# First head's rotation of two of three groups on VectorE, the high/low split of later heads asked for later, queries and keys low part first

## The chip, the cores and the metric

The kernel runs on one core of one Trainium2 chip. The metric is the time of one execution on the device in microseconds (us); of several runs the median counts. A core has five engines that run side by side, each with its own queue, which it works off in order: TensorE (PE; its weight loads PEld) multiplies matrices into PSUM, VectorE (DVE) and ScalarE (ACT) do elementwise work, GpSimd (POOL) too, but from SBUF alone here, and SyncE (SP) issues the transfers from HBM.

## What is computed

A decoder trunk of two layers over 256 tokens of width 1024. Layer 0 mixes tokens by a short gated convolution, layer 1 by dilated window attention; each is followed by a squared-ReLU MLP (1024 to 4096 and back) and a gated per-layer embedding. The change is in layer 1's attention, cut here to what matters:

```python
def dilated_attention_mixer(h, positions, w_qkv, w_o):       # 3 groups x 8 heads of 128
    qkv = (h @ w_qkv).reshape(b_, s_, 3, g_ * hh, dh)
    q = partial_rotary(qkv[:, :, 0], positions).reshape(b_, s_, g_, hh, dh)
    k = partial_rotary(qkv[:, :, 1], positions).reshape(b_, s_, g_, hh, dh)
    v = qkv[:, :, 2].reshape(b_, s_, g_, hh, dh)
    for g, (window, dilation) in enumerate(((128, 1), (512, 4), (2048, 16))):
        o_g, lse_g = dilated_window_attention(q[:, :, g], k[:, :, g], v[:, :, g], window, dilation)
    ...
    weights = jax.nn.softmax(jnp.stack(lses, axis=0), axis=0)
    o = jnp.sum(weights[..., None] * jnp.stack(outs, axis=0), axis=0)
    return o.reshape(b_, s_, hh * dh) @ w_o

def partial_rotary(x, positions):                            # the first 32 of a head's 128
    return concatenate([x1 * cos - x2 * sin, x2 * cos + x1 * sin, xf[..., ROPE_DIM:]])
```

## The kernel before

**Arithmetic.** Activations lie with channels on the partitions and tokens along the free dimension (`[128, 2, 256]` for two blocks of 128 channels). To keep float32 accuracy every operand of a large product is split into a high part, rounded to float32r, and a low part, the rest: ScalarE copies the high part (`whi` of weights, L332; activations in `split_into`, L405), VectorE subtracts (`wlo`, L281). A product is low weight times high activation plus high weight times both. In `block` (L343), for kind "w", that is two matmuls: `wlo` with 256 columns, and `whi` with 512 (high and low activation side by side), into one PSUM bank; `sums` (L381) adds the bank's halves at the end, ScalarE copying one half (L385), VectorE adding the other (L386). For the half `i` = 0 (queries) `wlo` comes first, for `i` = 1 (keys) `whi` (L358).

**Weights** come from HBM in slabs of 1024 columns (`raw`), five ahead; slab `si` + 5 is split when slab `si` is first used (`LOOK`). A head's queries and keys are two slabs per group, six in all, then four slabs of 768 columns for its values.

**The plan.** `make_plan` (L134) writes the order of all work as one list: matmul blocks, and steps (`("do", name, ...)`) between them. Instructions are recorded in this order, a scheduler puts them on each engine's queue by it, and waits are set where data is passed on. For the attention the plan goes head by head (L185 to L191): queries and keys of group 0, 1, 2 (`qk`; a group is 32 matmuls), each followed by `add_up` (out of PSUM) and `qk_out`; then values (`v`, 48 matmuls). The scores, the transposes (`turn`) and the product with the values (`values`) of head h - 1 stand between the blocks of head h. Head 0 is apart (L173 to L180): its three groups are accumulated side by side in three banks while the last gate is still being finished, then `add_up` of all three, the first two value blocks, `spread(3)` (which multiplies the norm's reciprocal into the tables `cosr` and `sinr`, L494 and L495), `qk_out` of the three groups, and the rest of the values. Head 1 is `late`: `scores(0)` stands after its third group, `turn(0)` after six of eight value steps, so 36 matmuls behind the scores.

**Rotation.** `qk_out(head, g)` (L607) is four GpSimd operations over query and key of a group, `t` of `[128, 512]`: times `cosr` (L609), two multiplies of 16 rows by `sinr` into the scratch tile `rot[g % 2]` (L612), and an addition of 48 rows (L618). For g = 0 it then asks for the split of `t` (`split_into`, L621), since group 0's scores are computed from high and low parts (L641); groups 1 and 2 go into the scores as they are (L644).

**Softmax of a head's scores** (`scores`, L635): VectorE adds the mask and takes the maximum (L647), negates it, ScalarE takes the exponential (L651; its table is loaded once before), VectorE the reciprocal, ScalarE scales (L653). `turn` (L656) transposes the result on TensorE (`tp`, L662).

Of the kernel before, what the change touches and what calls it, by code (L numbers as in the profile page):

```python
# [9 lines left out]
F32 = mybir.dt.float32  # L10
# [3 lines left out]
ALU = mybir.AluOpType  # L14
# [4 lines left out]
NK = D // P  # L19
# [3 lines left out]
GROUPS = 3  # L23
# [110 lines left out]
def make_plan():  # L134
    plan = [("do", "begin")]
    plan += proj_plan()
    for c in range(NP):
        for s, what in ((1, "C"), (2, "X"), (0, "B")):
            for k in range(NK):
                for i in (0, 1):  # L140
                    kind = "w" if what == "X" else "n"
                    plan.append((kind, "sc_in", k, s * NK + 2 * c + i, (what, c), i, "x0"))
                if c == 0 and (what, k) in ((("C", 3), ("C", 7), ("X", 1), ("X", 3))):
                    plan.append(("do", "squares", 0, (3, 7, 1, 3).index(k) if what == "C" else 2 + (k == 3)))
                if (c, what, k) == (0, "B", 2):
                    plan.append(("do", "stat", 0))
                if (c, what, k) == (1, "C", 4):
                    plan += [("do", "spread", 0), ("do", "conv", 0)]
            if what == "X":
                plan.append(("do", "add_up", (what, c)))  # L150
        if c:
            plan.append(("do", "conv", c))

    def mix(key, j, ks):
        return [("n", key, k, 2 * j + i, ("o", j), i, "y") for k in ks for i in (0, 1)]

    for k in range(6):
        plan += mix("sc_out", 0, (k,)) + mix("sc_out", 1, (k,))
    for j in range(NP):
        plan += mix("sc_out", j, range(6 if j < 2 else 0, NK)) + [("do", "mix_out", 0, j)]  # L160
    plan += mlp_plan(0) + gate_plan()

    plan.append(("do", "masks"))

    def qk(h, g, ks):
        return [
            ("w" if h else "n", "qkv", k, (i, g, h), ("qk", h, g), i, "x3") for k in ks for i in (0, 1)
        ]

    def v(h, ks):  # L170
        return [("t", "v", k, h, ("v", b, h), b, "x3") for k in ks for b in (0, 1)]

    for kp in range(NP):  # L173
        if kp == NP - 1:
            plan.append(("do", "stat", 3))
        for g in range(GROUPS):
            plan += qk(0, g, (2 * kp, 2 * kp + 1))
    plan += [("do", "add_up", ("qk", 0, g)) for g in range(GROUPS)]
    plan += v(0, (0, 1)) + [("do", "spread", 3)]
    plan += [("do", "qk_out", 0, g) for g in range(GROUPS)] + v(0, range(2, NK)) + [("do", "v_out", 0)]  # L180

    def sums(h, g):
        return [("do", "add_up", ("qk", h, g)), ("do", "qk_out", h, g)]

    for h in range(1, HEADS):  # L185

        late, steps = h == 1, [[("do", what, h - 1)] for what in ("scores", "turn", "values")]
        plan += qk(h, 0, range(NK)) + ([("do", "values", 0)] if h == 2 else []) + sums(h, 0)
        plan += [] if late else steps[0]
        plan += qk(h, 1, range(NK)) + sums(h, 1) + qk(h, 2, range(NK)) + steps[late ^ 1] + sums(h, 2)  # L190
        plan += v(h, range(6)) + steps[2 - late] + v(h, range(6, NK)) + [("do", "v_out", h)]  # L191

    last = HEADS - 1
    plan += [x for k in (0, 1, 2) for j in range(NP) for x in mix("w_o", j, (k,))]
    plan.append(("do", "scores", last))
    plan += [x for k in (3, 4) for j in range(NP) for x in mix("w_o", j, (k,))]
    plan.append(("do", "turn", last))
    plan += [x for k in (5, 6) for j in range(NP) for x in mix("w_o", j, (k,))]
    plan.append(("do", "values", last))
    for j in range(NP):  # L200
        plan += mix("w_o", j, (7,)) + [("do", "mix_out", 1, j)]
    plan += mlp_plan(1) + [("do", "last_load")] + last_plan()
    return plan
# [36 lines left out]
def tile_trunk(ctx: ExitStack, tc: tile.TileContext, plan, slabs, ap, out):  # L240
    nc = tc.nc
# [7 lines left out]
    def const(shape, name, dtype=F32):  # L249
        return cpool.tile(shape, dtype, tag=name, name=name)  # L250
# [4 lines left out]
    def held(tag, name, bufs=1, dtype=F32):  # L255
        return cpool.tile([P, 2, S], dtype, tag=tag, bufs=bufs, name=name)

    def pair(name, tag="pair", dtype=F32R):

        if tag == "pair":  # L260
            t = apool.tile([P, 2, 2, S], dtype, tag=tag, bufs=PAIR_BUFS, name=name)
        else:
            t = cpool.tile([P, 2, 2, S], dtype, tag=tag, bufs=1, name=name)
        return t[:, :, 0, :], t[:, :, 1, :], t
# [4 lines left out]
    def both(t):  # L269
        return t.unsqueeze(1).to_broadcast([P, 2, S])  # L270
# [17 lines left out]
    cosr = const([P, S], "cosr")  # L288
    sinr = const([P, S], "sinr")
    rot = [const([P, 2, S], f"rot{n}") for n in range(2)]  # L290
    pos = const([P, S], "pos", I32)
    h = [held("h", f"h{j}", NP + 1) for j in range(NP)]
    state = {k: {} for k in ("u", "y", "p0", "p1", "qk", "pT", *(f"x{n}" for n in range(6)))}
    acc, left, opened = {}, {}, set()
    for op in plan:
        if op[0] != "do":
            key = ((*op[4], op[5]), 0) if op[0] == "w" else (op[4], op[5] if op[0] == "n" else 0)
            left[key] = left.get(key, 0) + 1
    rstd, diags, rows, cur, mask, by_token = {}, {}, {}, {}, {}, {}
# [43 lines left out]
    def block(kind, key, k, col, name, half, operand, m=0, cuts=1):  # L343
        name = (*name, half) if kind == "w" else name
        if name not in opened:
            acc[name] = bank("acc_" + "_".join(map(str, name)))
        left[name, half if kind == "n" else 0] -= 1
        whi, wlo = weights((key, k, col))
        x = state[operand][k // 2]
        if kind == "n":  # L350
            dst = acc[name][:, half, :]
            products = ((dst, wlo, x[0][:, k % 2, :]), (dst, whi, x[1][:, k % 2, :]), (dst, whi, x[0][:, k % 2, :]))
        elif kind == "w":

            dst = acc[name]
            products = ((dst[:, 0, :], wlo, x[0][:, k % 2, :]), (flat(dst), whi, flat(x[2][:, k % 2, :, :])))

            products = products[::-1] if half else products  # L358
        else:
            n = width(key) * P // cuts  # L360
            whi, wlo = (t[:, m * n : (m + 1) * n] for t in (whi, wlo))
            dst = flat(acc[name])[:, :n]
            xhi, xlo = (t[:, k % 2, half * P : (half + 1) * P] for t in x[:2])
            products = ((dst, xhi, whi), (dst, xhi, wlo), (dst, xlo, whi))
        for n, (to, a, b) in enumerate(products):
            nc.tensor.matmul(  # L366
                to,
                a,
                b,
                start=n == 0 and name not in opened,  # L370
                stop=n == len(products) - 1 and left[name, half if kind == "n" else 0] == 0,
                skip_group_check=True,
            )
            opened.add(name)

    def close(name):
        opened.discard(name)

        return acc.pop(name)
# [21 lines left out]
    def split_into(kind, j, src, cuts=1):  # L401
        hi, lo, t = pair(f"{kind}{j}", "pp" if kind in ("p0", "p1") else "pair")
        for n in range(cuts):
            i = slice(2 * n // cuts, 2 * (n + 1) // cuts)
            nc.scalar.activation(hi[:, i, :], src[:, i, :], AF.Copy)  # L405
            sub(lo[:, i, :], src[:, i, :], hi[:, i, :])
        state[kind][j] = (hi, lo, t)
# [197 lines left out]
        h_ready(3, j)  # L605

    def qk_out(head, g):  # L607
        p, t = cur["qk", head, g]
        nc.gpsimd.tensor_tensor(t, p, both(cosr), ALU.mult)  # L609
        r = rot[g % 2]  # L610
        for src, dst in ((32, 0), (0, 32)):
            nc.gpsimd.tensor_tensor(  # L612
                r[dst : dst + 16],
                p[src : src + 16],
                sinr[src : src + 16].unsqueeze(1).to_broadcast([16, 2, S]),
                ALU.mult,
            )
        nc.gpsimd.tensor_tensor(t[:48], t[:48], r[:48], ALU.add)  # L618
        cur["qk", head, g] = t
        if g == 0:  # L620
            split_into("qk", head, t)  # L621

    def v_out(head):

# [130 lines left out]
    def last_scale(b, c):  # L755
# [6 lines left out]

    steps = dict(
        begin=begin, add_up=add_up, squares=squares, proj_out=proj_out, stat=stat, stat_rows=stat_rows, conv=conv, mix_out=mix_out, up_out=up_out,
        down_out=down_out, gate_out=gate_out, rope=rope, masks=masks_load, qk_out=qk_out, v_out=v_out,
        scores=scores, turn=turn, spread=spread, values=values,
        last_load=last_load, turn_h=turn_h, last_gate=last_gate, last_out=last_out, last_rms=last_rms, last_scale=last_scale,
    )
# [95 lines left out]
```

## Time and profile before

| | us |
|---|---|
| runs, median of 3 | 795.62 (795.31 to 795.94) |
| the profiled execution | 797.34 |
| its span, first to last instruction | 795.5 |
| TensorE busy in it | 776.2 (98%) |
| VectorE / ScalarE / GpSimd busy | 582.1 / 436.6 / 177.2 |
| head 1, up to head 2's first matmul (336.7 to 373.8 us) | 37.1 |
| each later head | 29.2 |

The profile is one execution. Its page sums the busy time of each engine; the views of the trace list instructions in order of time with the idle time before each and what ended it (`<-`), the waits of one engine on another, and the busy time and granted clock of a stretch. Times are from the start of the span. Layer 0 lasts to about 323 us, head 0's products overlap its end, heads 1 to 7 run to 550 us, and the second MLP, gate and last norm to the end.

### The profile page before, as it was taken

To read this page: it belongs to the slowest core of one execution; us is meant where nothing else is said; L and a number is where in the kernel's file an instruction comes from. 1 tells how busy PE (TensorE), PEld (TensorE's weight loads), DVE (VectorE), ACT (ScalarE), POOL (GpSimd) and SP (SyncE) were. 2 spreads that over 40 slices of the span, in tenths; PEclk is the share of its full clock that TensorE was granted. 3 is DMA by queue.
4 is the path that set the end of the run, shared out by engine and by line. 5 is a ranking of instruction groups with operands and counts; after the bars stand their busy time and mean duration, and the time that the engine had idled before them with its cause. 6 is when DMAs were issued, how large, how long until landed. Compare 5 with 4: busy or idle time off the path is not lost.

```text
span 795.5 us, 12797 instructions
## 1 busy us (share of the span) xinstructions
PE 776.2 (98%) x4986; PEld 711.6 (89%) x4986; DVE 582.1 (73%) x818; ACT 436.6 (55%) x672; POOL 177.2 (22%) x117
## 2 busy tenths in 40 slices
PE   8999999999999999996999999999999999999996
PEld 7999998888888999986999999999988888888985
DVE  6987789898556669747678679679598887555555
ACT  7654565565444447527647546646475555444453
POOL 0000000000000000298587677678000000000001
PEclk9999999999999999998999999999999999999999
DMA  8866555656556555643464455456556655555521
GB/s 277 287 211 193 183 187 181 198 187 196 185 186 188 185 163 168 203 128 115 150 186 144 154 180 159 159 159 200 174 159 189 198 188 191 185 185 189 184 78 54
DMA packets 41676, 140.98 MB, mean 177 GB/s; under 512 B 4752, under 2 KB 5136, under 8 KB 41616
## 3 DMA queue, kind: packets, MB, share of 16 engines
q1 hardware_dynamic: 41616, 140.17, 55.7%
q8 instruction: 39, 0.64, 0.3%
q14 instruction: 21, 0.17, 0.1%
HBM read 139.10 MB, written 1.05 MB: 176 GB/s over the span
## 4 chain that ended last, share of the span: by engine, by line
PE 87%; DVE 5%; POOL 3%; ACT 2%; issue 2%; DMA 1%; SPq 0%; POOLq 0%; DVEq 0%; ACTq 0%
PE acc_d L366 23%; PE acc_u L366 22%; PE acc_qk L366 13%; PE acc_v L366 7%; PE acc_o L366 6%; PE acc_g L366 5%; PE acc_B L366 2%; PE acc_X L366 2%; DVE wlo L281 2%; PE acc_C L366 2%; POOL rot L612 2%; PE tp L662 1%; PE o L683 1%; PE sc L644 1%; ACT whi L332 1%
## 5 line engine op out<-in xcount | busy, mean ns | idle before, releaser
L281 DVE TENSOR_TENSOR wlo<-raw,whi 128x1024 fp32r<-128x1024 f32 (+3 forms) x273 | 364.5, 1343 | 130.0 <-ACT whi L332 127.9
L332 ACT ACTIVATE whi<-raw 128x1024 fp32r<-128x1024 f32 (+3 forms) x273 | 276.3, 1018 | 201.4 <-PE acc_d L366 82.0
L366 PE MATMUL acc_d<-u,whi 128*128 128x512 f32 (+1 forms) x640 | 166.8, 351 | 0.0
L366 PE MATMUL acc_u<-x,whi 128*128 128x512 f32 x512 | 161.0, 396 | 0.0
L366 PE MATMUL acc_qk<-x,whi 128*128 128x512 f32 (+1 forms) x432 | 122.9, 371 | 0.0
L438 POOL TENSOR_TENSOR n<-v,power 128x4 f32<-128x4 f32 (+1 forms) x6 | 6.5, 1085 | 512.2 <-DVE v L458 509.4
L366 PEld LDWEIGHTS acc_u<-x,wlo 128*128 128x128 f32 x512 | 96.4, 188 | 22.4
L366 PEld LDWEIGHTS acc_d<-u,wlo 128*128 128x128 f32 x512 | 96.9, 189 | 17.0
L366 PE MATMUL acc_d<-u,wlo 128*128 128x256 f32 x512 | 111.8, 279 | 0.0
L366 PE MATMUL acc_u<-x,wlo 128*128 128x256 f32 x512 | 101.3, 278 | 0.0
L366 PEld LDWEIGHTS acc_d<-u,whi 128*128 128x128 f32 x640 | 98.5, 190 | 0.0
L612 POOL TENSOR_TENSOR rot<-qk,sinr 16x512 f32<-16x512 f32 x48 | 87.0, 1813 | 3.3
L366 PEld LDWEIGHTS acc_qk<-x,wlo 128*128 128x128 f32 x384 | 72.4, 188 | 14.2
L366 PE MATMUL acc_qk<-x,wlo 128*128 128x256 f32 x384 | 82.5, 281 | 0.0
L366 PEld LDWEIGHTS acc_u<-x,whi 128*128 128x128 f32 x512 | 78.0, 189 | 0.1
L366 PE MATMUL acc_v<-whi,x 128*128 128x384 f32 x256 | 69.8, 343 | 0.0
L366 PEld LDWEIGHTS acc_qk<-x,whi 128*128 128x128 f32 x432 | 66.1, 189 | 0.0
L609 POOL TENSOR_TENSOR qk<-qk,cosr 128x512 f32<-128x512 f32 x24 | 37.9, 1578 | 57.9 <-DVE qk L386 44.6
L366 PEld LDWEIGHTS acc_v<-whi,x 128*128 128x128 f32 x256 | 47.4, 191 | 0.0
L366 PE MATMUL acc_o<-y,whi 128*128 128x256 f32 x256 | 46.0, 284 | 0.0
L366 PE MATMUL acc_v<-wlo,x 128*128 128x384 f32 x128 | 43.3, 339 | 0.0
L618 POOL TENSOR_TENSOR qk<-qk,rot 48x512 f32<-48x512 f32 x24 | 42.8, 1784 | 1.7
(164 smaller groups left out, 1029.6 us busy)
## 6 DMA issues: line engine op xcount, KB each, us to landing
raw<-in_w SPq DMA_DIRECT2D x232, 512.0 KB, 3.7
raw<-in_w SPq DMA_DIRECT2D x32, 384.0 KB, 3.1
raw<-in_w SPq DMA_DIRECT2D x7, 256.0 KB, 5.7
h<-in_xT SPq DMA_DIRECT2D x4, 256.0 KB, 6.0
out<-ht SPq DMA_DIRECT2D x4, 256.0 KB, 2.0
pt<-in_pT SPq DMA_DIRECT2D x2, 256.0 KB, 4.6
mask<-in_mask SPq DMA_DIRECT2D x2, 256.0 KB, 4.3
gain<-in_gain SPq DMA_DIRECT2D x2, 256.0 KB, 4.2
```

What stands on the lines that cost most here:

```text
L281: nc.vector.tensor_tensor(out, a, f32(b), ALU.subtract)
L332: nc.scalar.activation(hi[:, :width], t[:, :width], AF.Copy)
L366: nc.tensor.matmul(to, a, b, start=n == 0 and name not in opened, stop=n == len(products) - 1 and left[name, half if kind == "n" else 0] == 0,
L438: nc.gpsimd.tensor_tensor(y, v, power[:, : v.shape[1]], ALU.pow)
L609: nc.gpsimd.tensor_tensor(t, p, both(cosr), ALU.mult)
L612: nc.gpsimd.tensor_tensor(r[dst : dst + 16], p[src : src + 16], sinr[src : src + 16].unsqueeze(1).to_broadcast([16, 2, S]), ALU.mult,)
L618: nc.gpsimd.tensor_tensor(t[:48], t[:48], r[:48], ALU.add)
L644: nc.tensor.matmul(ps[:, (g + 1) * P : (g + 2) * P], t[:, 0, own], t[:, 1, own], start=True, stop=True)
L662: nc.tensor.transpose(ps[n // 2][:, n % 2, b * P : (b + 1) * P], sm[:, n * P : (n + 1) * P], ident)
L683: nc.tensor.matmul(ps[:, 0, b * P : (b + 1) * P], v12[:, b, g * P : (g + 1) * P], t[:, g, b * P : (b + 1) * P], start=False, stop=g == 1, ...
```

## The change

Four edits, all in the attention. The first head's groups 0 and 1 are no longer copied out of PSUM by ScalarE; `qk_out` finds their bank still open and does the same four operations on VectorE, reading PSUM (`engine`). Group 2 is copied and rotated on GpSimd as before, first of the three in the plan. The scratch tile is `rot[0]` for groups 0 and 1 and `rot[1]` for group 2. The split of group 0 is a step of its own, `qk_split`: for head 0 it stands after the first sums of head 1, for head h from 1 on after three of eight value steps instead of right after `qk_out(h, 0)`. And `block` no longer turns the order round for the keys.

```diff
-    plan += [("do", "add_up", ("qk", 0, g)) for g in range(GROUPS)]
+    plan.append(("do", "add_up", ("qk", 0, 2)))
     plan += v(0, (0, 1)) + [("do", "spread", 3)]
-    plan += [("do", "qk_out", 0, g) for g in range(GROUPS)] + v(0, range(2, NK)) + [("do", "v_out", 0)]
+    plan += [("do", "qk_out", 0, g) for g in (2, 0, 1)] + v(0, range(2, NK)) + [("do", "v_out", 0)]
...
-        plan += [] if late else steps[0]
+        plan += [("do", "qk_split", 0)] if late else steps[0]
         plan += qk(h, 1, range(NK)) + sums(h, 1) + qk(h, 2, range(NK)) + steps[late ^ 1] + sums(h, 2)
-        plan += v(h, range(6)) + steps[2 - late] + v(h, range(6, NK)) + [("do", "v_out", h)]
+        plan += v(h, range(3)) + [("do", "qk_split", h)] + v(h, range(3, 6)) + steps[2 - late]
+        plan += v(h, range(6, NK)) + [("do", "v_out", h)]
...
-            products = products[::-1] if half else products
+            products = products[::-1] if half and key != "qkv" else products
...
     def qk_out(head, g):
-        p, t = cur["qk", head, g]
-        nc.gpsimd.tensor_tensor(t, p, both(cosr), ALU.mult)
-        r = rot[g % 2]
+        if ("qk", head, g) in acc:
+            engine, p, t = nc.vector, close(("qk", head, g)), pair(f"qk_{head}_{g}", dtype=F32)[1]
+        else:
+            engine, (p, t) = nc.gpsimd, cur["qk", head, g]
+        engine.tensor_tensor(t, p, both(cosr), ALU.mult)
+        r = rot[g // 2]
         for src, dst in ((32, 0), (0, 32)):
-            nc.gpsimd.tensor_tensor(
+            engine.tensor_tensor(
...
-        nc.gpsimd.tensor_tensor(t[:48], t[:48], r[:48], ALU.add)
+        engine.tensor_tensor(t[:48], t[:48], r[:48], ALU.add)
         cur["qk", head, g] = t
-        if g == 0:
-            split_into("qk", head, t)
+
+    def qk_split(head):
+        split_into("qk", head, cur.pop(("qk", head, 0)))
```

What this does to VectorE's queue behind `cosr` and `sinr` is seen first of before, then of the change. In the names `qk_0_1` is head 0, group 1, `acc_...` its PSUM bank, `qk0` and `qk1` the split of a head's group 0; the last number is the tile's own.

```order
L494 TENSOR_TENSOR cosr_78<-cosr_78,row_3_3694 128x256
L495 TENSOR_TENSOR sinr_79<-sinr_79,row_3_3694 128x256
L281 TENSOR_TENSOR wlo124_3734<-raw124_3588,whi124_3733 128x1024
L281 TENSOR_TENSOR wlo125_3752<-raw125_3635,whi125_3751 128x1024
L281 TENSOR_TENSOR qk0_3702<-qk_0_0_3665,qk0_3702 128x2x256
L630 SCALAR_TENSOR_TENSOR v0_0_3767<-acc_v_0_0_3671,n2_3_3613,v0_0_3767 128x128
L630 SCALAR_TENSOR_TENSOR v0_0_3767<-acc_v_1_0_3681,n2_3_3613,v0_0_3767 128x128
```

```order
L495 TENSOR_TENSOR cosr_78<-cosr_78,row_3_3690 128x256
L496 TENSOR_TENSOR sinr_79<-sinr_79,row_3_3690 128x256
L613 TENSOR_TENSOR qk_0_0_3698<-acc_qk_0_0_3465,cosr_78 128x2x256
L616 TENSOR_TENSOR rot0_80<-acc_qk_0_0_3465,sinr_79 16x512 x2
L613 TENSOR_TENSOR qk_0_1_3703<-acc_qk_0_1_3484,cosr_78 128x2x256
L622 TENSOR_TENSOR qk_0_0_3698<-qk_0_0_3698,rot0_80 48x2x256
L282 TENSOR_TENSOR wlo124_3729<-raw124_3588,whi124_3728 128x1024
L616 TENSOR_TENSOR rot0_80<-acc_qk_0_1_3484,sinr_79 16x512 x2
L282 TENSOR_TENSOR wlo125_3747<-raw125_3635,whi125_3746 128x1024
```

Eight operations of the rotation come in ahead of and between the two weight splits, and head 0's split leaves this place.

On ScalarE, from a weight copy of the second head to the table load of the first exponential, of before and then of the change:

```order
L332 ACTIVATE whi129_3859<-raw129_3749 128x768
L405 ACTIVATE qk1_3830<-qk_1_0_3821 128x2x256
L385 ACTIVATE qk_1_1_3879<-acc_qk_1_1_0_3833 128x256
L332 ACTIVATE whi130_3891<-raw130_3776 128x768
L385 ACTIVATE qk_1_1_3879<-acc_qk_1_1_1_3842 128x256
L332 ACTIVATE whi131_3914<-raw131_3799 128x1024
L385 ACTIVATE qk_1_2_3964<-acc_qk_1_2_0_3888 128x256
L332 ACTIVATE whi132_3976<-raw132_3834 128x1024
L385 ACTIVATE qk_1_2_3964<-acc_qk_1_2_1_3897 128x256
L651 ACT_TABLE_LOAD
```

```order
L333 ACTIVATE whi129_3854<-raw129_3744 128x768
L386 ACTIVATE qk_1_1_3874<-acc_qk_1_1_0_3828 128x256
L386 ACTIVATE qk_1_1_3874<-acc_qk_1_1_1_3837 128x256
L333 ACTIVATE whi130_3886<-raw130_3771 128x768
L333 ACTIVATE whi131_3909<-raw131_3794 128x1024
L386 ACTIVATE qk_1_2_3959<-acc_qk_1_2_0_3883 128x256
L406 ACTIVATE qk1_4000<-qk_1_0_3816 128x2x256
L386 ACTIVATE qk_1_2_3959<-acc_qk_1_2_1_3892 128x256
L333 ACTIVATE whi132_3971<-raw132_3829 128x1024
L656 ACT_TABLE_LOAD
```

The split of head 1 (`qk1`) moves from ahead of the sums of groups 1 and 2 to between the two sums of group 2, still ahead of the table load.

## Rows read from the trace of the kernel before

**Rows 1.** The page, busy us, share of the span and instructions of TensorE

```profile
PE 776.2 (98%) x4986; PEld 711.6 (89%) x4986; DVE 582.1 (73%) x818; ACT 436.6 (55%) x672; POOL 177.2 (22%) x117
```

**Rows 2.** TensorE's waits in the whole program: us in total, times, longest

```profile
PE tp L662 <- ACT sm L653: 7.0, 1, 7.0
```

**Rows 3.** TensorE in order of time, second head: start us, us, engine, line, operation

```profile
353.43 0.51 PE L641 MATMUL sc<-qk 128*128 128x256 f32 x3
...
355.35 0.42 PE L366 MATMUL acc_v<-whi,x 128*128 128x384 f32 x1
...
368.81 1.97 PE L662 MATMUL tp<-ident,sm 128*128 128x128 f32 x8 [6.97 <-ACT sm L653]
370.43 0.67 PE L366 MATMUL acc_v<-whi,x 128*128 128x384 f32 x1
...
373.78 0.28 PE L366 MATMUL acc_qk<-x,wlo 128*128 128x256 f32 x1
```

**Rows 4.** The same view, a later head: scores and transposes

```profile
410.10 0.51 PE L641 MATMUL sc<-qk 128*128 128x256 f32 x3
...
411.62 0.36 PE L366 MATMUL acc_qk<-x,wlo 128*128 128x256 f32 x1
...
422.87 1.04 PE L662 MATMUL tp<-ident,sm 128*128 128x128 f32 x8
423.66 0.42 PE L366 MATMUL acc_v<-whi,x 128*128 128x384 f32 x1
```

**Rows 5.** The chain that ended last, in order of time: start us, us, what

```profile
382.71 11.16 PE acc_qk L366 x64
...
423.91 6.24 PE acc_v L366 x36
...
431.75 2.08 PE acc_v L366 x12
...
439.76 0.45 PE sc L644 x4
```

**Rows 6.** Stretch: us, busy PE, PEld, DVE, ACT, POOL, then granted clock, DMA

```profile
370.40:372.90 2.50, 2.50 (x10) 2.50 (x9) 2.50 (x2) 2.50 (x4) 2.42 (x2) 0.50 0.00 0
```

**Rows 7.** GpSimd, ScalarE, VectorE in order of time, heads 0 and 1

```profile
333.28 1.34 POOL L609 TENSOR_TENSOR qk<-qk,cosr 128x512 f32<-128x512 f32 x1 [7.95 <-DVE cosr L494]
...
334.69 4.38 POOL L612 TENSOR_TENSOR rot<-qk,sinr 16x512 f32<-16x512 f32 x2
...
358.26 1.27 POOL L618 TENSOR_TENSOR qk<-qk,rot 48x512 f32<-48x512 f32 x1
359.56 0.63 ACT L405 ACTIVATE qk<-qk 128x512 fp32r<-128x512 f32 x1 [12.07 <-POOL qk L618]
...
360.23 0.69 DVE L281 TENSOR_TENSOR qk<-qk,qk 128x512 fp32r<-128x512 f32 x1 [8.47 <-ACT qk L405]
```

**Rows 8.** ScalarE in order of time, ahead of head 0's exponentials

```profile
362.57 1.06 ACT L332 ACTIVATE whi<-raw 128x1024 fp32r<-128x1024 f32 x1
...
363.93 1.28 ACT L651 ACT_TABLE_LOAD   x1
365.22 0.72 ACT L651 ACTIVATE sm<-sm,st 128x512 f32<-128x512 f32 x1
```

**Rows 9.** VectorE's groups by form: xcount, busy us, mean ns of one

```profile
L595 DVE TENSOR_TENSOR gs<-acc_g,row 128x512 f32<-128x512 f32 x4 | 2.8, 688 | 0.0
```

**Rows 10.** VectorE in order of time, first part of the second head

```profile
342.39 1.23 DVE L281 TENSOR_TENSOR qk<-qk,qk 128x512 fp32r<-128x512 f32 x1 [4.46 <-ACT qk L405]
...
344.06 3.77 DVE L281 TENSOR_TENSOR wlo<-raw,whi 128x1024 fp32r<-128x1024 f32 x2
347.75 0.41 DVE L386 TENSOR_TENSOR qk<-acc_qk,qk 128x256 f32<-128x256 f32 x1
```

**Rows 11.** GpSimd and ScalarE in order of time, a later head

```profile
437.02 2.15 POOL L618 TENSOR_TENSOR qk<-qk,rot 48x512 f32<-48x512 f32 x1
...
447.10 0.63 ACT L405 ACTIVATE qk<-qk 128x512 fp32r<-128x512 f32 x1 [3.40 <-POOL qk L618]
```

More of the change, by code (lines that the diff above doesn't have):

```diff
@@ L764, in tile_trunk @@
         begin=begin, add_up=add_up, squares=squares, proj_out=proj_out, stat=stat, stat_rows=stat_rows, conv=conv, mix_out=mix_out, up_out=up_out,
-        down_out=down_out, gate_out=gate_out, rope=rope, masks=masks_load, qk_out=qk_out, v_out=v_out,
+        down_out=down_out, gate_out=gate_out, rope=rope, masks=masks_load, qk_out=qk_out, qk_split=qk_split, v_out=v_out,
         scores=scores, turn=turn, spread=spread, values=values,
```

## Prediction

> **What bounds the kernel now.** I read the page first: TensorE is busy for 776.2 us of the span, 98% [rows 1]. So only time in which TensorE stands still, or runs slower than elsewhere, can be won. The list of its waits over the whole program has one large entry: 7.0 us, once, before the transposes `tp`, ended by ScalarE's `sm` [rows 2]. TensorE's instructions in time show the place [rows 3]: it is the second head (h = 1), where the scores of head 0 are computed (353.43), then 36 value matmuls, then the transposes, then 12 more value matmuls, then head 2's queries and keys (373.78). From the scores to head 2 these four pieces took 373.78 - 353.43 = 20.35 us. A later head does the same four pieces without a wait: scores 411.62 - 410.10 = 1.52, transposes 423.66 - 422.87 = 0.79 [rows 4], 36 matmuls 6.24 and 12 matmuls 2.08 [rows 5], together 10.63 us. **So 9.72 us are lost here**: 0.40 in the scores (355.35 - 353.43 = 1.92 for 1.52), 7.22 before the transposes (355.35 + 6.24 = 361.59, start at 368.81), and 0.83 + 1.27 after them (1.62 for 0.79, and 3.35 for 2.08), where the granted clock was 0.50 [rows 6], which is 1.2 of 2.4 GHz.
>
> Why it waits is read on GpSimd, ScalarE and VectorE [rows 7]. GpSimd starts head 0's first group at 333.28 and turns four groups (three of head 0, the first of head 1) one after the other; the fourth ends at 358.26 + 1.27 = 359.53. ScalarE's high-part copy of head 1's first group stood at the front of its queue from 347.5 on and waited 12.07 us for exactly that. Everything behind it waited too: the sums of head 1's second and third group, weight copies, the exponentials of head 0's scores. VectorE waited 8.47 us for the same copy, with head 0's mask step behind it. Then ScalarE caught up: table load at 363.93, first exponential at 365.22 [rows 8], transposes at 368.81.
>
> **The change part by part.** (1) *Groups 0 and 1 of head 0 move to VectorE, read from PSUM.* GpSimd loses eight of the sixteen operations ahead of that ScalarE copy; ScalarE loses two PSUM copies that lay beside other work (worth nothing). VectorE gains eight operations. No row shows this one on VectorE from PSUM with 16 partitions. Bounds: the nearest row, PSUM times an SBUF row at 128x512, is 0.69 us [rows 9]; the dearest of that width, two SBUF operands beside a busy GpSimd, is 1.23 [rows 10], against 0.69 for the same split with GpSimd idle [rows 7]. I take no discount for 16 rows: on GpSimd 16 rows cost 2.19 (4.38 for two [rows 7]) and 48 rows 2.15 [rows 11]. A sum out of PSUM of 256 columns stays at 0.41 while GpSimd runs [rows 10], so the six PSUM operations get 0.69, and of the two additions one gets 1.23 and one 0.69: 4.1 + 1.9 = 6.0 us (ends: 5.5 and 9.8). What hides it: VectorE was idle 4.46 us just there, up to 342.39 [rows 10], and the weight splits that it pushes back are not due. The first of them belongs to the second half of head 1's second group. TensorE starts head 1's keys and queries 3 x 5.58 = 16.7 us before 353.43 (a group is half of 11.16 [rows 5]), at 336.7, and reaches that half 1.5 groups later, at 345.1. The PSUM banks that are held longer are next written by head 1's third group, from 347.9, when VectorE has long read them.
>
> Now the clock of the new order. VectorE starts at 333.3 (where the same `cosr` released GpSimd [rows 7]). Up to the sums of head 1's first group it has 6.0 us of rotation, four short steps out of PSUM at 0.41 at most (1.6), and four weight splits: 3.77 for two beside GpSimd [rows 10], and with GpSimd idle, by the ratio 0.69 to 1.23, an estimated 2.1 for two. 333.3 + 7.6 + 4.2 to 7.5 = 345.1 to 348.4. GpSimd, with one group of head 0 left, is free by 338.4 to 342.1 (four operations cost 4 x 1.27 = 5.1 alone and 2 x 4.38 = 8.8 beside VectorE [rows 7]). So it starts head 1's first group at 345.1 and needs 5.1 to 8.8: 350.2 to 353.9, at the worst end of both 357.2. I take 353.8, the contended price after the early start: VectorE is busy with splits then, but GpSimd was idle before.
>
> (2) *The split is asked for later.* ScalarE's high part of head 1 now stands behind the sum of the third group's queries, which TensorE ends half a four (below) before 353.43, at 353.1: it runs at 353.8 instead of holding up the queue from 347.5. But it stands ahead of head 0's exponentials, with a sum, a weight copy and the table load: 0.63 [rows 7], 0.4 like its VectorE half [rows 10], 1.06 and 1.28 [rows 8]; first exponential at 357.2. From the first exponential to the transposes it took 368.81 - 365.22 = 3.59 us [rows 3, 8], with the same VectorE steps in between: 360.8. TensorE, no longer waiting in the scores, arrives at 353.43 + 1.52 + 6.24 = 361.19. Margin 0.4 us: **no wait**, and the clock does not fall. Head 0's own split no longer depends on GpSimd and runs several us before the scores.
>
> For heads 2 to 7 the same move takes a wait of 3.40 us off ScalarE [rows 11], but TensorE waits for nothing there [rows 2], so it is worth nothing.
>
> (3) *Low part first for queries and keys.* The number of instructions and columns is the same; only the second half of each four is turned round. A four takes 4 x 11.16 / 64 = 0.698 us [rows 5]; at the pace of the value matmuls (384 columns, the same mean, 6.24 / 36 = 0.1733 [rows 5]) it would take 0.693. 168 fours times 0.0048 is 0.8 us: I take 0, with 0.8 either way.
>
> **The sum.** Profiled span 795.5 - 9.72 = 785.8; its execution 797.34 - 9.72 = 787.6. The median of the runs shown, 795.62, is 1.7 below the profiled execution; on it the same gain gives 795.62 - 9.72 = **785.9 us**.
>
> **The rivals.** *A new wait takes the old one's place.* The margin of 0.4 us is small against the spread of GpSimd's end (350.2 to 357.2). If head 1's first group ends at 357.2, the first exponential starts at 360.6, the transposes at 364.2: 3.0 us of the gain are lost, 788.9; if the clock falls as it did, another 2.1. For it: all engines but TensorE are denser there than before. Against: it takes the worst price at each step.
>
> *GpSimd's third group comes late in every head, and the kernel gets slower.* Now that group's last addition ends at 437.02 + 2.15 = 439.17 [rows 11], and the part of the scores that reads it starts at 439.76 [rows 5]: 0.6 us to spare. The change puts VectorE's low part of the split (two SBUF operands) beside just this rotation. Were nothing else to move and GpSimd lost the whole 1.23 us of it, 0.6 us a head would be lost, 3.8 in six heads: 789.7. It decides against the change from 2.2 us late per head on (0.6 to spare and 9.72 / 6 = 1.6): 796 or more. Against it: GpSimd already pays the contended price in that rotation (2.15 for 1.27), and the sums that feed its second group no longer stand behind ScalarE's 3.40 us, so it starts earlier. The rule in the Trainium skill's page "SBUF — State Buffer", section "Who interferes with whom", speaks for this rival: a VectorE instruction with two SBUF inputs and a GpSimd instruction that reads SBUF exclude each other, the later one for the whole length of the first. By that page, as an estimate, each split would cost GpSimd its whole 0.69 us, just above what is to spare; that the trace has 2.15 for 1.27 agrees in kind.
>
> *The rotation wasn't the cause.* If the transposes were late by the exponentials' own length, only the 0.40 us in the scores would come back: 795.2. Against: ScalarE's wait of 12.07 us ends on GpSimd by name.
>
> **How the numbers follow.** Forecast 0.64 (785.9, own range 784.9 to 786.9 from the 0.8 and the runs' spread of 0.6); new wait 0.23 (786.9 to 788.9, rarely 791); GpSimd late but short of the break-even 0.07 (up to 794), past it 0.03; not the cause 0.03. A measurement of this kernel tells about 0.2% from no change, 1.6 us. Faster 0.64 + 0.23 + 0.07 = 0.94, same 0.03, slower 0.03. The range 784.9 to 789.0 holds the first two cases but for their tails.
>
> **What would show it.** Right: no wait of TensorE on `sm` before `tp` in the second head, granted clock 1.00 throughout, head 2's queries at about 364.1; ScalarE's split of head 1 waiting under 1 us; VectorE's rotations at 0.6 to 0.7 us each from PSUM. Wrong: a wait before `tp` with GpSimd's addition behind it, waits of the scores on GpSimd in each later head, waits on weight low parts near 345, or a pace of the query and key matmuls other than 11.16 us for 64.

## The result, and the profile after

| | before | after |
|---|---|---|
| runs beside each other, median | 795.78 us (795.31 to 796.26) | 785.75 us (785.33 to 787.43) |
| the profiled execution | 797.34 | 785.7 |
| its span | 795.5 | 783.9 |

The ratio is 0.9876, 95% interval 0.9864 to 0.9887: the kernel is 10.0 us faster. The forecast was 785.9.

The page's busy times, and TensorE's waits in the whole program (us in total, times, longest), of the changed kernel. Lines of the code move on by one up to L607 and by five behind.

```profile
PE 773.3 (99%) x4986; PEld 709.5 (91%) x4986; DVE 574.5 (73%) x826; ACT 438.2 (56%) x670; POOL 167.5 (21%) x109
```

```profile
PE warm L506 <- DVE power L502: 1.0, 1, 1.0
...
PE acc_p L367 <- DVE wlo L282: 0.3, 1, 0.3
```

The wait of 7.0 us before the transposes [rows 2] is gone, and no wait of the scores has come. TensorE in order of time, second head, the lines that answer to [rows 3]:

```profile
351.76 0.51 PE L646 MATMUL sc<-qk 128*128 128x256 f32 x3
...
353.27 0.42 PE L367 MATMUL acc_v<-whi,x 128*128 128x384 f32 x1
...
359.63 1.04 PE L667 MATMUL tp<-ident,sm 128*128 128x128 f32 x8
360.42 0.42 PE L367 MATMUL acc_v<-whi,x 128*128 128x384 f32 x1
...
362.61 0.28 PE L367 MATMUL acc_qk<-x,wlo 128*128 128x256 f32 x1
```

From the scores to head 2 it is 362.61 - 351.76 = 10.85 us, where it was 20.35: **9.50 us came from this place**. The granted clock of the two stretches around the transposes (us; busy PE, PEld, DVE, ACT, POOL; clock; DMA share and GB/s) is full, where [rows 6] had 0.50:

```profile
353.40:361.30 7.90, 7.90 (x51) 7.86 (x50) 5.40 (x12) 7.12 (x12) 7.61 (x6) 1.00 0.29 96
361.30:364.20 2.90, 2.90 (x19) 2.73 (x18) 2.90 (x3) 2.90 (x7) 2.84 (x2) 1.00 0.40 127
```

The rest came from the pace of queries and keys: 64 matmuls in the chain take 11.11 us for 11.16 [rows 5], which over seven heads is 0.5 to 0.6 us.

```profile
371.52 11.11 PE acc_qk L367 x64
```

All times of this profile are some 1.7 us earlier than those of before (scores 351.76 for 353.43; in layer 0's MLP it is 1.6 already), which is no part of the change. In the profiled execution of before TensorE waited longer for a weight split at the start, 2.2 us where the changed kernel's shows 0.3; the row of before:

```profile
PE acc_p L366 <- DVE wlo L281: 2.2, 3, 1.4
```

It is probably why that execution stood 1.7 us above its median; no other execution of before has a trace. Together 9.50, 0.5 to 0.6 and 1.6 make the 11.6 us between the two spans. Below, 1.7 is taken off a forecast clock time before it is compared.

VectorE, GpSimd and ScalarE in order of time, heads 0 and 1, of the changed kernel: the rotation from PSUM, the first group of head 1, its split, the mask steps and the exponentials (to set beside [rows 7, 8, 10]):

```profile
331.79 0.68 DVE L613 TENSOR_TENSOR qk<-acc_qk,cosr 128x512 f32<-128x512 f32 x1
332.48 1.38 DVE L616 TENSOR_TENSOR rot<-acc_qk,sinr 16x512 f32<-16x512 f32 x2
...
333.10 2.64 POOL L616 TENSOR_TENSOR rot<-qk,sinr 16x512 f32<-16x512 f32 x2
...
334.50 1.78 DVE L622 TENSOR_TENSOR qk<-qk,rot 48x512 f32<-48x512 f32 x1
...
340.00 0.68 DVE L622 TENSOR_TENSOR qk<-qk,rot 48x512 f32<-48x512 f32 x1
...
343.94 3.42 POOL L613 TENSOR_TENSOR qk<-qk,cosr 128x512 f32<-128x512 f32 x1 [5.37 <-DVE qk L387]
...
350.77 2.14 POOL L622 TENSOR_TENSOR qk<-qk,rot 48x512 f32<-48x512 f32 x1
...
352.95 0.63 ACT L406 ACTIVATE qk<-qk 128x512 fp32r<-128x512 f32 x1 [0.95 <-POOL qk L622]
...
354.63 0.68 DVE L652 CUSTOM_DVE_ANT_0 sm<-sc,mask 128x512 f32<-128x512 f32 x1
...
356.11 0.73 ACT L656 ACTIVATE sm<-sm,st 128x512 f32<-128x512 f32 x1
...
358.39 1.34 ACT L658 ACTIVATE sm<-sm,st 128x512 f32<-128x512 f32 x2 [0.76 <-DVE st L657]
```

GpSimd now waits for its input (5.37 us) ahead of head 1's first group, where it had come to it with a backlog, and ScalarE's split waits 0.95 us instead of 12.07.

### The profile page after: what moved, and what is told of

It reads as the page before. It is cut to its first block, busy times and chain, and to the rows that moved or that the text cites. A ratio compares the mean times of both kernels' runs of the same rounds, so it can differ in the third digit from the quotient of the medians.

```text
span 783.9 us, 12761 instructions
## 1 busy us (share of the span) xinstructions
PE 773.3 (99%) x4986; PEld 709.5 (91%) x4986; DVE 574.5 (73%) x826; ACT 438.2 (56%) x670; POOL 167.5 (21%) x109
## 4 chain that ended last, share of the span: by engine, by line
PE 93%; DVE 3%; issue 1%; ACT 1%; DMA 1%; SPq 0%; POOL 0%; POOLq 0%; DVEq 0%; ACTq 0%
PE acc_d L367 23%; PE acc_u L367 23%; PE acc_qk L367 15%; PE acc_v L367 9%; PE acc_o L367 6%; PE acc_g L367 4%; PE acc_B L367 3%; PE acc_X L367 3%; PE acc_C L367 3%; PE o L688 1%; PE sc L649 1%; PE tp L667 1%; DVE wlo L282 1%; PE sc L646 1%; PE o L682 1%
## 5 line engine op out<-in xcount | busy, mean ns | idle before, releaser
L282 DVE TENSOR_TENSOR wlo<-raw,whi 128x1024 fp32r<-128x1024 f32 (+3 forms) x273 | 350.3, 1289 | 160.4 <-ACT whi L333 158.0
L367 PE MATMUL acc_qk<-x,whi 128*128 128x512 f32 (+1 forms) x432 | 134.5, 368 | 0.0
L367 PE MATMUL acc_qk<-x,wlo 128*128 128x256 f32 x384 | 107.8, 281 | 0.0
L367 PEld LDWEIGHTS acc_qk<-x,whi 128*128 128x128 f32 x432 | 77.8, 188 | 13.6
L616 POOL TENSOR_TENSOR rot<-qk,sinr 16x512 f32<-16x512 f32 x44 | 78.3, 1780 | 3.0
```

The source lines that it names most:

```text
L282: nc.vector.tensor_tensor(out, a, f32(b), ALU.subtract)
L367: nc.tensor.matmul(to, a, b, start=n == 0 and name not in opened, stop=n == len(products) - 1 and left[name, half if kind == "n" else 0] == 0,
L616: engine.tensor_tensor(r[dst : dst + 16], p[src : src + 16], sinr[src : src + 16].unsqueeze(1).to_broadcast([16, 2, S]), ALU.mult,)
```

## The experiments

Two theories stood against each other. By Q both things count: when GpSimd is through with head 1's first group, and where ScalarE's split stands in its queue. By G only GpSimd's backlog counts, and the split may be asked for where it likes. The low part first was run by itself too, and in more forms later, since its runs did not do what the count of columns says. The scratch tile's new number and group 2 as the first of the plan go with the rotation in every run; they were not tried by themselves. The runs of before beside these had medians of 795.94 (first four experiments), 796.30 (next four) and 795.99 us (last two).

**The three edits apart and together.**

| rotation | split later | low first | us | ratio to before, 95% interval |
|---|---|---|---|---|
| | | x | 797.52 | 1.0023 [1.0013, 1.0032] |
| | x | | 793.31 | 0.9965 [0.9951, 0.9979] |
| x | | | 787.95 | 0.9903 [0.9888, 0.9918] |
| x | | x | 788.17 | 0.9903 [0.989, 0.9917] |
| x | x | | 786.38 | 0.9876 [0.9863, 0.989] |
| x | x | x | 785.75 | 0.9876 [0.9864, 0.9887] |

**Low part first alone.** The kernel before, with this edit:

```diff
-            products = products[::-1] if half else products
+            products = products[::-1] if half and key != "qkv" else products
```

> The kernel before with only the third edit: queries and keys low part first, nothing else. Theory: 64 query and key matmuls of later heads take 11.11 us instead of 11.16 (as in the trace of the changed kernel), so 32 take 0.025 to 0.03 less, 21 groups of 32 together 0.5 to 0.6 us; the wait of 7.0 us before the transposes stays. Time 0.5 to 0.6 us under the kernel before (ratio 0.9993). Rival: the order costs nothing either way and the 0.05 us belong to the other edits; ratio 1.0000.

Measured: 797.52, 1.6 us slower than before. The pace came as expected (11.10 us for 64 matmuls), but the wait before the transposes grew from 7.0 to 8.7 us. VectorE, GpSimd, ScalarE and TensorE in order of time in this run:

```profile
359.91 3.17 DVE L281 TENSOR_TENSOR wlo<-raw,whi 128x768 fp32r<-128x768 f32 x2
...
360.07 1.93 POOL L609 TENSOR_TENSOR qk<-qk,cosr 128x512 f32<-128x512 f32 x1 [2.13 <-DVE qk L386]
...
363.67 0.67 DVE L647 CUSTOM_DVE_ANT_0 sm<-sc,mask 128x512 f32<-128x512 f32 x1
...
364.28 2.32 DVE L281 TENSOR_TENSOR wlo<-raw,whi 128x1024 fp32r<-128x1024 f32 x1
366.52 0.14 DVE L650 TENSOR_SCALAR st<-st 128x1 f32<-128x1 f32 x1
...
366.69 0.72 ACT L651 ACTIVATE sm<-sm,st 128x512 f32<-128x512 f32 x1 [3.08 <-DVE st L650]
...
368.97 1.97 PE L662 MATMUL tp<-ident,sm 128*128 128x128 f32 x8 [8.73 <-ACT sm L653]
```

The edit turns matmuls round, and the scheduler then places other instructions elsewhere too. A weight split of 2.32 us now stands between head 0's mask step and its negation, and the exponential waits for the negation. Ahead of it, the two sums of a group come as a pair, so GpSimd starts its next group at 360.07, beside the two weight splits (one of 768 and one of 1024 columns; the row names the first), which take 3.17 us for 0.96 and 1.23 in the kernel before. ScalarE's split starts at 357.97 here; from there to the transposes it is 11.00 us, where before has 368.81 - 359.56 = 9.25 [rows 3, 7]: 1.75 us are lost here. Less the 0.5 to 0.6 that the pace gives, this is 1.2 of the measured 1.6; the other 0.4 stay open. That the order is the cause is read from this chain; the same edit with the order held still was not run.

**Rotation alone.** The changed kernel with the split asked for in `qk_out` again and the keys high part first.

> Only the first edit: groups 0 and 1 of head 0 on VectorE from PSUM; every split is asked for where the kernel before asks, keys high part first. Theory Q (ScalarE's queue order and GpSimd's end both count): head 1's first group ends some 5 us earlier on GpSimd, and ScalarE's split with it, but the sums and weight copies still queue behind it, so the first exponential moves from 365.2 to about 360.2 and the transposes from 368.8 to 363.8, against TensorE's arrival at 361.2: a wait of 2.6 us is left, 7.1 us are gained, 5.0 if the clock falls; about 788.5 to 790.7. Theory G (GpSimd's load alone counts): all of it is gained, about 786.2.

Measured: 787.95, a wait of 1.22 us before the transposes, between the two expectations. ScalarE and TensorE:

```profile
351.85 0.63 ACT L406 ACTIVATE qk<-qk 128x512 fp32r<-128x512 f32 x1 [7.12 <-POOL qk L622]
...
357.51 0.73 ACT L655 ACTIVATE sm<-sm,st 128x512 f32<-128x512 f32 x1
...
361.16 1.27 PE L666 MATMUL tp<-ident,sm 128*128 128x128 f32 x8 [1.22 <-ACT sm L657]
```

GpSimd lets go of the split 7.7 us earlier than in [rows 7] (of which 1.5 is this execution's earlier clock), but the split still holds ScalarE's queue for 7.12 us, and what it held up is worked off ahead of the exponential: 5.66 us from split to exponential, 3.16 in the changed kernel.

**Later split alone.** The kernel before, with `qk_split` as in the change.

> Only the second edit: the splits asked for later, as in the change; all rotations on GpSimd, keys high part first. Theory Q: ScalarE's split of head 1 still waits for GpSimd's fourth group until 359.5, but only the table load stands between it and the exponentials: first exponential at 361.4, transposes at 365.0 against an arrival of TensorE at 361.6, a wait of 3.4 us; 5.9 us are gained, 3.8 if the clock falls, and GpSimd's backlog may take 0 to 2 more at the scores of head 1: 789.8 to 793.5. Theory G: the release by GpSimd has not moved, so nothing is gained but under 1 us: 795.

Measured: 793.31, at the dear end of Q. TensorE's waits (the second is that of head 0's scores for GpSimd's third group), the value matmuls behind the transposes in the chain (2.08 in a later head), and the granted clock there:

```profile
PE tp L664 <- ACT sm L655: 2.7, 1, 2.7
...
PE sc L646 <- POOL qk L619: 1.7, 1, 1.7
```

```profile
366.56 3.35 PE acc_v L367 x12
```

```profile
365.00:369.80 4.80, 4.80 (x21) 4.60 (x22) 3.30 (x2) 4.69 (x7) 4.64 (x4) 0.64 0.02 6
```

ScalarE's queue is free, but GpSimd still has four groups ahead of the split (it ends the fourth at 360.80), and the split stands ahead of the exponentials: 2.7 us are left, and the clock falls behind them as it did before.

**Only head 1's split moved out of the way.** The kernel before, with the split of head 1 alone asked for behind the transposes of head 0:

```diff
-        if g == 0:
+        if g == 0 and head != 1:
             split_into("qk", head, t)
...
-        plan += v(h, range(6)) + steps[2 - late] + v(h, range(6, NK)) + [("do", "v_out", h)]
+        plan += v(h, range(6)) + steps[2 - late] + ([("do", "qk_split", 1)] if late else [])
+        plan += v(h, range(6, NK)) + [("do", "v_out", h)]
```

> The kernel before with one step moved: head 1's split of group 0 is asked for behind head 0's transposes instead of right after its rotation; GpSimd keeps all of head 0. Theory Q: no exponential waits for GpSimd's fourth group; only the scores wait 0.4 us for the third. No wait before the transposes, 9.3 us gained at this place; but GpSimd is 16 operations behind, head 1's third group ends at 372 to 377 against 371.8 for head 1's scores, so 0 to 5 us come back as a new wait there: 786.4 to 791.5. Theory G: GpSimd's load is what counts, so under 1 us is gained: 795.

Measured: 794.39, ratio 0.9979 [0.997, 0.9988]: 1.55 us gained, outside both expectations, and nearer to G's 795 than to Q's dear end of 791.5. TensorE's waits, then GpSimd and TensorE at head 1's scores, and the chain behind:

```profile
PE sc L648 <- POOL qk L619: 5.4, 2, 4.7
```

```profile
374.85 1.86 POOL L619 TENSOR_TENSOR qk<-qk,rot 48x512 f32<-48x512 f32 x1
...
376.76 0.49 PE L648 MATMUL sc<-qk 128*128 128x128 f32 x2 [4.66 <-POOL qk L619]
```

```profile
378.60 12.18 PE acc_qk L367 x64
```

The wait before the transposes is gone, and it comes back 15 us later: head 1's scores wait for GpSimd's third group of head 1. That is the new wait which Q had named, at its upper end of 5 us; besides, head 0's scores wait 0.73 us, and the clock falls behind the 4.66 us (12.18 for 11.16), which Q had not counted. So the backlog is the cause, and the queue is where it showed first. At neither of the two places tried did asking later replace taking the work off GpSimd; that the queue counts too is shown by the 1.22 us that the rotation alone leaves.

**Rotation and later split, without the low part first.**

> The changed kernel without its last edit: the keys have their high part first again, as before. If the low part first is worth its pace and no more, head period 29.16 in place of 29.08 and 11.16 in place of 11.11 for 64 query and key matmuls, together 0.5 to 0.6 us: 786.3. No wait before the transposes of the second head, since both other edits are in. If the order that comes with the edit counts as in the run of the low part alone (there 1.7 us at the second head), the mask steps stand elsewhere here too (a weight split between the second mask step and its negation, the low part of head 1's split behind them), and the transposes wait up to 2 us: 786.5 to 788.5, or earlier than in the changed kernel by as much as it had lost, below 785.7.

Measured: 786.38, as expected from the pace. The times alone do not tell it from the changed kernel: beside its own runs of before each has the ratio 0.9876. The traces, one of each, do, by 0.6 us of span (784.5 and 783.9) and the chain:

```profile
371.58 11.16 PE acc_qk L367 x64
```

**Rotation and low part first, split early.**

> Rotation on VectorE and low part first, the split asked for early as before. With it the three edits are there alone and in pairs. If low part first is worth its pace alone: 787.4 (0.5 under the rotation alone, 787.95), the wait before the transposes 1.2 us as there. If the order counts that comes with it (on VectorE a weight split between head 0's first mask step and its negation, behind it the first exponential), 1.2 to 2.8 us of that split come on top of the wait: 788.6 to 790.2, a wait of 2.4 to 4.0.

Measured: 788.17, between the two. The gain of pace is there (11.11), and the wait is 1.91 instead of 1.22 us, since the weight split stands between mask and negation here too:

```profile
357.95 1.22 DVE L282 TENSOR_TENSOR wlo<-raw,whi 128x1024 fp32r<-128x1024 f32 x1
359.09 0.14 DVE L654 TENSOR_SCALAR st<-st 128x1 f32<-128x1 f32 x1
...
359.27 0.72 ACT L655 ACTIVATE sm<-sm,st 128x512 f32<-128x512 f32 x1 [2.00 <-DVE st L654]
```

It costs less than in the run of the edit alone, 1.22 us for 2.32. Only together with the later split, which leaves 0.6 us to spare at the transposes, is the low part first a gain, and that by the traces.

**GpSimd's third group made longer.** The changed kernel, with the two multiplies of 16 rows done twice in the third group of heads 1 to 7:

```diff
-        for src, dst in ((32, 0), (0, 32)):
+        for src, dst in ((32, 0), (0, 32)) * (2 if g == 2 and head else 1):
```

> The changed kernel, and GpSimd multiplies the 16 rows of each third group by the sine twice over in heads 1 to 7 (the same values again): 2 more operations a head, 3.2 to 4.4 us. The rival in which GpSimd's third group comes late had 0.6 us to spare per head, by the kernel before: then 2.6 to 3.8 us late in each of six heads, 801 to 809. By the trace of the changed kernel the third group of a later head ends 4.4 us ahead of the scores that read it (423.82 and 428.26) and that of head 1 2.5 us ahead (367.55 and 370.02): no wait of the later heads or under 0.3 us each, at head 1 0.7 to 1.9: 786.4 to 788.5.

Measured: 790.01, ratio 0.9923 [0.991, 0.9937]. It is 4.3 us above the changed kernel, 1.5 more than the dear end of the margins of its trace, and far from the 801 of the rival. GpSimd in a later head of this run, and of the changed kernel:

```profile
419.57 8.85 POOL L616 TENSOR_TENSOR rot<-qk,sinr 16x512 f32<-16x512 f32 x4
428.50 1.88 POOL L622 TENSOR_TENSOR qk<-qk,rot 48x512 f32<-48x512 f32 x1
```

```profile
417.21 4.37 POOL L616 TENSOR_TENSOR rot<-qk,sinr 16x512 f32<-16x512 f32 x2
421.66 2.16 POOL L622 TENSOR_TENSOR qk<-qk,rot 48x512 f32<-48x512 f32 x1
```

The two operations cost 8.85 - 4.37 = 4.48 us, and each head takes 0.4 to 0.6 us longer (head 1 1.5), of which TensorE's listed waits for GpSimd's third group are 0.16 to 0.35 (1.25 in head 1). So the changed kernel has some 4 us to spare at a place where before had 0.6 [rows 5, 11].

**Low part first everywhere.** The changed kernel without the exception for other keys:

```diff
-            products = products[::-1] if half and key != "qkv" else products
```

> The changed kernel with the low part first in every block of this kind, so also in the second MLP and the mixer's output product (the changed kernel turns the order round there still). If the pace is what alternating 256 and 512 columns gives wherever they stand (0.05 us for 64 matmuls, as read in queries and keys: 168 fours gave 0.5 to 0.6), some 480 fours that are turned round besides give 1.3 to 1.8 us: 784.0 to 784.5. If the gain is peculiar to the attention, 785.7. If the scheduler's order changes at a place that waits, above 785.7.

Measured: 790.22, ratio 0.9917 [0.9904, 0.9931], 4.5 us above the changed kernel. The first MLP in the chain of this run, and one of queries and keys, then the first MLP of the changed kernel (the second MLP's up block takes 67.84 for 66.89 too):

```profile
128.95 67.84 PE acc_u L366 x384
196.79 90.87 PE acc_d L366 x576
...
374.32 11.11 PE acc_qk L366 x64
```

```profile
128.10 66.89 PE acc_u L367 x384
194.99 89.92 PE acc_d L367 x576
```

TensorE waited no longer than in the changed kernel; the matmuls themselves are slower, with the same instructions and columns. Per pair (one of 256 and one of 512 columns) it is 67.84 / 192 = 0.3533 us for 0.3484, while queries and keys gained, 11.11 / 32 = 0.3472 for 0.3488.

**High part first.** Queries and keys high part first on both halves (785.76, ratio 0.9873 [0.9858, 0.9888]), and every block of this kind high part first (789.36, ratio 0.9912 [0.9891, 0.9932]):

```diff
-            products = products[::-1] if half and key != "qkv" else products
+            products = products[::-1] if half or key == "qkv" else products
```

```diff
-            products = products[::-1] if half and key != "qkv" else products
+            products = products[::-1]
```

> The changed kernel with the high part first, in place of the low part, for queries and keys of both halves: 512 and 256 columns alternate as there, only what stands first is turned. If the alternation alone makes the pace of 11.11 us for 64 matmuls (start to start 230 and 117 ns), it is 11.11 here too, head period 29.08, 785.7 to 786.4 (the sums of the queries can come a matmul earlier or later). If what stands first decides into which rhythm the matmuls fall, another pace: up to the 353 ns a pair that the up and down blocks showed with the low part first everywhere, 6 ns more for each of 336 pairs: 787.7.

> High part first in every block of this kind, so alternating in the up, down and X blocks too, with the 512 columns first. With the low part first everywhere the up and down blocks kept a round of three pairs (241, 120, 236, 113, 233, 117 ns, 353 a pair) against 349 a pair with equal ones side by side, and the kernel took 790.2. If the order of the first two decides, up and down fall into the rhythm of queries and keys (347 a pair): 784 to 785. If the place decides (operands, banks, what the other engines do there), 353 a pair stays: 790 to 791.

The chain of the first, then of the second:

```profile
371.32 11.10 PE acc_qk L367 x64
```

```profile
128.82 67.84 PE acc_u L367 x384
```

For queries and keys, and for the first MLP, what stands first does not matter; alternating does: queries and keys gain, the MLP loses. One block breaks this rule. The first 128 matmuls of the second MLP's up block, with the low part first everywhere and then with the high part first everywhere (22.50 us in the changed kernel):

```profile
569.65 22.27 PE acc_u L366 x128
```

```profile
569.52 22.86 PE acc_u L367 x128
```

It gains in the one run and loses in the other, so the kind of block does not decide. The four executions of the last run took 787.8, 788.0, 790.7 and 790.8 us, two near the dear expectation of 790 to 791 and two some 3 us faster; the trace is of the slowest, and what the faster two did is not shown. No version that was run beats the changed kernel: 785.76 is the same.

## Why the prediction was right

**What bounds the kernel** was read rightly: 9.50 of the 9.72 us that were counted as lost came back. The 0.22 that seem to stay are the value matmuls, 359.63 - 353.27 = 6.36 for 6.24 and 362.61 - 360.42 = 2.19 for 2.08. But the sum set times from start to start beside times of the chain, which are shorter: from start to start a later head of before takes 6.33 and 2.17 too. Read in one way throughout (1.52 + 6.33 + 0.79 + 2.17 = 10.81), 20.35 - 10.81 = 9.54 us were lost, and nearly all of it came back.

**Step 1, rotation on VectorE**, was forecast at 6.0 us and took 0.68 + 1.38 + 0.69 + 1.78 + 1.38 + 0.68 = 6.59. The six from PSUM took 0.69 each as taken; one addition was dearer (1.78 for 1.23). The idle time of VectorE hid it. The last of the eight operations, the second addition, ran at 340.00, behind both weight splits and not ahead of or between them. GpSimd began head 1's first group at 343.94 (forecast 345.1, less 1.7: 343.4) and needed 8.97 us (forecast up to 8.8): it ended at 352.91, where 353.8 less 1.7 was expected, so 0.8 late.

**Step 2, the later split.** ScalarE's split waited 0.95 us, and the first exponential ran at 356.11 (forecast 357.2 less 1.7: 355.5). The first scaling was done at about 358.39 + 1.34 / 2 = 359.06, and TensorE arrived at 359.63: a margin of 0.6 us, forecast 0.4. The 0.6 that the exponential was late came back behind it, because the scheduler put both mask steps ahead of the weight split, which the step had not counted on. The margin does not hang on it: without the low part first, where a weight split stands between the second mask step and its negation, the first exponential runs at 355.10, the scaling starts at 358.42 and TensorE arrives at 359.69, 0.6 us to spare again. The step said that asking later is worth nothing in heads 2 to 7: true of the time. But the third group of a later head now ends at 421.66 + 2.16 = 423.82, 4.4 us ahead of the scores that read it (428.26), where 0.6 us was to spare: about the wait of 3.40 us [rows 11] that it took off ScalarE. The runs show that the later split makes this room: with it alone the third group ends 3.6 us ahead (431.97 and 435.60), with the rotation alone 0.1 us (430.06 and 430.19).

**Step 3, low part first**, was taken as 0 with 0.8 either way. It gave 0.05 us for 64 matmuls, 0.5 to 0.6 in all. So two terms of the sum were mis-sized, 9.72 for 9.5 and 0 for 0.5 to 0.6, one too high and one too low: 9.50 + 0.5 to 0.6 is 10.0 to 10.1 for a measured 10.0. That the forecast of 785.9 came within 0.2 us is in part luck. Another pace than 11.16 was among the prediction's own signs of being wrong; it was so in this term alone. The step was also too narrow: it counted columns only, and the edit alone moved VectorE's queue and cost 1.75 us at the second head.

**The rivals.** The new wait did not come, though its row was close: without the later split it is there (1.22 us), and with the split moved but the backlog left, it comes at another place (4.66 us). GpSimd's third group did not come late: the rival gave it 0.6 us to spare, and the changed kernel has 4; with the rotation alone, at 0.1 us, it was near. The rotation was the cause: alone it gave 8.0 of 10.0 us. The rotation from PSUM took 0.68 us while GpSimd was multiplying beside it; the addition with two SBUF inputs took 1.78 us there and 0.68 with GpSimd idle. The Trainium skill's page "SBUF — State Buffer", section "Who interferes with whom", says that a VectorE instruction with at most one SBUF input, outside its two-port modes, does not contend with GpSimd, and that one with two contends with a GpSimd instruction that reads SBUF: this trace agrees with both.

## What to carry to other kernels

When an in-order queue waits for a slow engine, look for the backlog behind it: moving the waiting instruction mostly moved the wait here (1.6 and 2.6 us gained of 10), taking work off the slow engine into another's idle time removed most of it (8.0), and the two together left a margin. An edit that only reorders matmuls can change the order that a scheduler makes for the other engines; compare these queues where the kernel waits, before crediting it with its pace. Measure an order of matmuls at each place where it is used: the same alternation gained in one block and lost in another.

## What the runs showed of the hardware

**Alternating matmuls fall into steady rounds.** From start to start in the traces, queries and keys with alternating columns keep 230 and 117 ns, or vary a little around that (230 to 233 and 112 to 118); both are 347 a pair. The first MLP's up and down blocks in the same order keep a round of three pairs, 241, 120, 236, 113, 233, 117 ns, 353 a pair, through 384 matmuls each. With equal ones side by side the round has eight, near 233, 236, 116, 113, 232, 231, 113, 119 ns, 348 a pair. The granted clock is 1.00 and the instructions are the same. The same code fell into either round: with the low part first everywhere the second MLP's up block began at 347 a pair and the first MLP's at 353, and of layer 0's four X blocks, 32 matmuls each, one took 5.56 us and the others 5.64 or 5.65 (5.58 in the changed kernel). What decides the round stays open: neither what stands first nor the kind of block does it alone; operands' and banks' places and the work of the other engines were not varied.

**The granted clock behind a wait of TensorE.** Behind the wait of 1.91 us it stayed at 1.00, which is 2.4 GHz. Behind 2.75 us it was 0.64 in the mean of 4.80 us, in which both levels stand: 1.00 up to 365.6 us, 0.50, which is 1.2 GHz, from 366.2 to 369.0, and 1.00 again from 369.6. Behind 4.66 us it was 0.50 from 378.0 to 380.6, and 64 matmuls took 12.18 us for 11.16. The first is this stretch of the run with rotation and low part first:

```profile
363.00:366.00 3.00, 3.00 (x19) 2.87 (x19) 2.92 (x2) 3.00 (x6) 2.94 (x2) 1.00 0.00 0
```
